# A decoder layer whose x and first weights arrive interleaved, and whose small loads leave POOL's queue

## The chip, the cores and the metric

The kernel runs on one core of a Trainium2 chip. The core's engines have instruction queues of their own: PE (TensorE, matrix multiply, with its weight loads shown as PEld), DVE (VectorE), ACT (ScalarE), POOL (GpSimd) and SP (SyncE, which here only issues transfers). All transfers run on the core's 16 DMA engines. The metric is the device time of one execution in microseconds; lower is better.

## The reference

One layer over 256 positions of width 1024, in float32. The input is normed and multiplied with one wide matrix; its columns are the queries, keys and values of three kinds of attention and three gates. The attention outputs are projected, gated, summed, projected again and added to x; then come a second norm and an MLP with a short convolution.

```
h = rmsnorm(x, ln1);  z = h @ w_in
qa, ka, va, qb, kb, vb, fb, qc, kc, vc, ga, gb, gc = split(z)
o_a = block-sparse attention(qa, ka, va) with a position bias
o_b = forgetting attention(qb, kb, vb, fb + b_f)
o_c = sliding-window attention(qc, kc, vc, sinks) with a position bias
x = x + (sigmoid(ga)*(o_a @ w_pa) + sigmoid(gb)*(o_b @ w_pb) + sigmoid(gc)*(o_c @ w_pc)) @ w_o
u = causal_conv3(rmsnorm(x, ln2) @ w_up);  a, b = split(u)
out = rmsnorm(x + (silu(a) * b) @ w_down, ln_f)
```

## The kernel before

Each float32 product is made of three fast products: an operand is split into a high part, which ACT writes in the fast type, and a low part, the rest, which DVE subtracts; PE adds high times high, low times high and high times low. Weights come as pieces of up to 128 rows by 1024 columns (512 KB). The class `Weights` takes each piece through three steps, in the order of use: "load" (SP issues the transfer into one of five `raw` buffers), "hi" (ACT, L109) and "lo" (DVE, L116). A piece holds for 512 output columns two blocks of 128 of the contraction index. The first four pieces are cut finer.

The row norm is not applied to h before the first products. Their left operand is x, transposed and times the gain ln1, in eight blocks of 128 by 256 (`hThi` and `hTlo`, L308 to L314); the scale of the norm, computed from the untransposed x (`xt`) by four ACT squares (L276), a short chain on DVE and ACT and a product with a diagonal matrix (`diag`, L282, and PE's L289), is multiplied in as the results leave PSUM. The products follow each other as groups: first qB and kB (four pieces, L394), then v1 (values and forget logits of the B heads, three pieces, L243 to L245), then qA and kA (four pieces; the first is called m0 below), v2, qC and so on.

The order of the work around PE's products is written by a planner (`filler`, `step`): each product adds its cost to a running clock, and other tasks are put between the products when the clock reaches their time in the table `AT` (norm, positions, mm, gates and others). An engine runs its instructions in the order in which they are written. ACT and DVE splits stand some pieces ahead of the product that uses them.

At the start SP issues transposed x (`in_xT`) and the first four pieces by turns: the gain with block 0 of x, two quarters of the first piece, block 1 of x, the rest of the piece, then x by two blocks and weights by half pieces (L167 to L193). Transposed x lies in `G`, which later serves other purposes. POOL, having made three constant masks, issues five small loads (L218 to L222): the position bias table (`relx`, two parts, and `oneh`), the forget bias (`bfb`) and the sinks (`skb`). PE runs seven products of zeros until its first operands are there. At most eight of SP's transfers are under way at once, since each waits for the one eight before it.

Of the kernel before, what the change touches and what calls it, by code (L numbers as in the profile page):

```python
# [7 lines left out]
F32 = mybir.dt.float32  # L8
F32R = mybir.dt.float32r
# [46 lines left out]
class Weights:  # L56

    def __init__(self, nc, pool, pieces):  # L60
        self.nc, self.pool, self.pieces = nc, pool, pieces
        self.raw, self.parts = {}, {}
# [74 lines left out]


@with_exitstack
def hybrid_kernel(ctx: ExitStack, tc: tile.TileContext, x, xT, ln_f, w_main, w_v1, w_v2, b_f, sinks,  # L140
                  rel_bias, onehot, cols, out):
# [38 lines left out]
    load_x(2, 4)  # L180
    W.load_to(2)
    load_x(4, 6)
    W.load_to(3)
    load_x(6, 8)
    W.load_to(4)
    cv = const.tile([P, 192], F32, name="cv")[:, :4 * 2 * NF + KD]
# [60 lines left out]
    def small(shape, name, bufs=2):  # L247
        return act.tile([P] + shape, F32, name=name, tag=name, bufs=bufs)
# [73 lines left out]
    for _ in range(2):  # L322
        W.step("lo")
    W.step("hi")
    low()
    W.step("lo")
    for k in range(2, 8, 2):
        lows = [x_hi(k), x_hi(k + 1)]
        W.hi_to(k // 2 + 1)
        for low in lows:  # L330
            low()
        W.prep_to(k // 2 + 1)
# [6 lines left out]
    def spawn(task, when=0.0):  # L339
        tasks.append((when, task))  # L340
# [111 lines left out]
    def group_v1():  # L452
# [429 lines left out]
    for j in range(NF):  # L882
# [12 lines left out]
        hi = ml.tile([P, S], F32R, name="ah", tag="ah", bufs=TAIL + 2)  # L895
        lo = ml.tile([P, S], F32R, name="al", tag="al", bufs=TAIL + 2)
# [149 lines left out]
```

## Time and profile before

| | us |
|---|---|
| median of 3 runs (range) | 388.01 (387.05 to 389.1) |
| the profiled execution | 388.68 |
| its span, first to last instruction | 387.0 |
| PE busy | 377.2 (97%) |
| DVE, ACT, POOL busy | 287.7, 230.7, 8.0 |

The share of busy time is a mean over stages with different limits. In the chain each piece of time belongs to what the last instruction in the end waited for; where the chain is all PE, only fewer or faster matmuls shorten the program, and where it names a transfer or another engine, PE stood still. The granted clock is 1.00 at TensorE's higher level, 2.4 GHz, and 0.50 at its lower, 1.2 GHz. A row's duration of a matmul overlaps the next one's; the step from one to the next is what counts.

### The profile page before, as it was taken

How to read it: one execution, taken by the hardware profiler on the slowest of the kernel's cores; microseconds unless marked ns; L12 is line 12 of the kernel's file. 1: busy time of each engine (PE TensorE's matmuls, PEld its weight loads, DVE VectorE, ACT ScalarE, POOL GpSimd, SP SyncE). 2: the span in 40 equal slices, each digit the busy share in tenths (PEclk: the TensorE clock that was granted, in tenths of full speed). 3: DMA queues.
4: the chain of work that ended last, by engine and by line, in shares of the span. 5: the costliest groups of instructions: out<-in, count | busy, mean ns of one | idle time of the engine just before them, and what ended most of it. 6: DMA issues, size and time to landing. Idle time of an engine off the chain costs nothing.

```text
span 387.0 us, 6530 instructions
## 1 busy us (share of the span) xinstructions
PE 377.2 (97%) x2464; PEld 340.1 (88%) x2464; DVE 287.7 (74%) x540; ACT 230.7 (60%) x399; POOL 8.0 (2%) x20
## 2 busy tenths in 40 slices
PE   6999999999999999999999999999999999999993
PEld 6999999787887888888899999999999999999983
DVE  3785967574856717967778999878887878888745
ACT  4883464665757685336587767556655656656433
POOL 4010000000000000000000000000000000000000
PEclk9899999999999999999999999999999999999998
DMA  7999765344552637444736567655565556463002
GB/s 197 402 331 334 279 181 181 130 130 149 170 172 90 218 108 233 151 160 119 262 108 222 204 224 223 216 196 186 170 213 180 201 171 205 171 218 109 2 0 108
DMA packets 21374, 70.86 MB, mean 183 GB/s; under 512 B 2504, under 2 KB 3413, under 8 KB 21344
## 3 DMA queue, kind: packets, MB, share of 16 engines
q1 hardware_dynamic: 20448, 68.05, 52.1%
q0 software_dynamic: 752, 2.18, 1.7%
q8 instruction: 19, 0.31, 0.4%
q10 hardware_dynamic: 144, 0.23, 0.2%
q14 instruction: 11, 0.09, 0.1%
HBM read 69.38 MB, written 1.07 MB: 182 GB/s over the span
## 4 chain that ended last, share of the span: by engine, by line
PE 96%; DMA 1%; DVE 1%; SPq 0%; ACT 0%; issue 0%; DVEq 0%
PE s L834 16%; PE acc L243 16%; PE acc L244 15%; PE acc L245 15%; PE pt L834 8%; PE o L834 8%; PE acc L394 7%; PE pt L394 2%; PE s L619 2%; PE o L394 1%; DMA raw<-in_w_main 1%; PE s L566 1%; PE s L608 1%; PE s L301 0%; PE pt L566 0%; PE pt L773 0%
## 5 line engine op out<-in xcount | busy, mean ns | idle before, releaser
L116 DVE TENSOR_TENSOR wlo<-raw,whi 128x1024 fp32r<-128x1024 f32 (+4 forms) x131 | 150.3, 1161 | 17.4 <-ACT whi L109 17.4
L109 ACT ACTIVATE whi<-raw 128x1024 fp32r<-128x1024 f32 (+4 forms) x131 | 129.1, 1005 | 49.2 <-PE acc L244 24.6
L243 PE MATMUL acc<-whi,hThi 128*128 128x512 f32 (+2 forms) x160 | 61.3, 383 | 0.0
L244 PE MATMUL acc<-whi,hTlo 128*128 128x512 f32 (+2 forms) x160 | 59.8, 374 | 0.0
L245 PE MATMUL acc<-wlo,hThi 128*128 128x512 f32 (+2 forms) x160 | 59.8, 374 | 0.0
L834 PE MATMUL s<-oThi,whi 128*128 128x256 f32 x176 | 49.3, 281 | 0.0
L834 PE MATMUL s<-oThi,wlo 128*128 128x256 f32 x176 | 49.2, 280 | 0.0
L834 PE MATMUL s<-oTlo,whi 128*128 128x256 f32 x176 | 48.9, 280 | 0.0
L842 ACT ACTIVATE ya<-v,cv 128x256 f32<-128x256 f32 x22 | 13.3, 603 | 42.7 <-DVE v L839 42.7
L243 PEld LDWEIGHTS acc<-whi,hThi 128*128 128x128 f32 x160 | 30.1, 188 | 6.0 <-issue 1.3
L245 PEld LDWEIGHTS acc<-wlo,hThi 128*128 128x128 f32 x160 | 30.0, 188 | 5.1
L244 PEld LDWEIGHTS acc<-whi,hTlo 128*128 128x128 f32 x160 | 30.1, 188 | 4.7 <-DVE hTlo L295 0.2
L244 PE MATMUL acc<-whi,al 128*128 128x512 f32 (+1 forms) x88 | 33.8, 384 | 0.0
L245 PE MATMUL acc<-wlo,ah 128*128 128x512 f32 (+1 forms) x88 | 33.8, 384 | 0.0
L243 PE MATMUL acc<-whi,ah 128*128 128x512 f32 (+1 forms) x88 | 33.8, 384 | 0.0
L834 PEld LDWEIGHTS s<-oTlo,whi 128*128 128x128 f32 x176 | 33.5, 191 | 0.0
L834 PEld LDWEIGHTS s<-oThi,wlo 128*128 128x128 f32 x176 | 33.0, 188 | 0.4
L834 PEld LDWEIGHTS s<-oThi,whi 128*128 128x128 f32 x176 | 33.0, 188 | 0.4
L834 PE MATMUL pt<-oThi,whi 128*128 128x256 f32 x88 | 24.8, 282 | 0.0
L834 PE MATMUL pt<-oThi,wlo 128*128 128x256 f32 x88 | 24.7, 281 | 0.0
L834 PE MATMUL pt<-oTlo,whi 128*128 128x256 f32 x88 | 24.7, 281 | 0.0
L834 PE MATMUL o<-oThi,whi 128*128 128x256 f32 x88 | 24.7, 281 | 0.0
(243 smaller groups left out, 749.0 us busy)
## 6 DMA issues: line engine op xcount, KB each, us to landing
raw<-in_w_main SPq DMA_DIRECT2D x115, 512.0 KB, 3.8
raw<-in_w_main SPq DMA_DIRECT2D x7, 256.0 KB, 5.6
raw<-in_w_v SPq DMA_DIRECT2D x4, 384.0 KB, 3.9
xt<-in_x SPq DMA_DIRECT2D x2, 512.0 KB, 6.9
G<-rowsd POOLq DMA_DIRECT2D x1, 1024.0 KB, 12.6
raw<-in_w_v SPq DMA_DIRECT2D x2, 390.0 KB, 6.2
G<-in_xT SPq DMA_DIRECT2D x3, 256.0 KB, 6.1
out_y<-xt SPq DMA_DIRECT2D x2, 288.0 KB, 2.2
```

The source lines that it names most:

```text
L109: self.nc.scalar.activation(self.parts[i][0][:, cs], self.raw[i][:, cs], AF.Copy)
L116: self.nc.vector.tensor_sub(lo[:, cs], self.raw[i][:, cs], hi[:, cs].bitcast(F32))
L243: nc.tensor.matmul(o, lh, rh, start=start, stop=False, **kw)
L244: nc.tensor.matmul(o, ll, rh, start=False, stop=False, **kw)
L245: nc.tensor.matmul(o, lh, rl, start=False, stop=stop, **kw)
L394: nc.tensor.matmul(o, w[:, kk, cs], hT[h][:, k, :], start=first, stop=last, skip_group_check=True)
L566: nc.tensor.matmul(sc[2 * i + e][:, lo:lo + m], q[h, qi, qs], k[h, ki, 0:m], start=True, stop=True)
L608: nc.tensor.transpose(pts[h][:, i * P:(i + 1) * P], L[:, h, i * P:(i + 1) * P], ident)
L619: nc.tensor.matmul(os[i][e * HD:(e + 1) * HD, cs], v[t][:, vi, e, :], p[:, S:ROWS] if t else p[:, 0:S], start=t == 0, stop=t == 1, **kw)
L834: nc.tensor.matmul(u, w, h2T[h][:, k, :], start=k == 0 and i == 0, stop=k == KD - 1 and i == 2)
L842: nc.scalar.activation(y, v, AF.Identity, scale=w[2], bias=w[3])
```

## The change

The host packs gain, transposed x and the first four pieces into one array `head`: 8 columns of gain, then four blocks of 1536 columns, each x block 2i, piece i, x block 2i+1. SP loads it in nine transfers into a buffer `begin` of its own, cut at columns 512, 1024, 1536 and then every 768. The pieces count as loaded, so the five `raw` buffers are free for what follows. The bias table becomes one array `table` of 34 rows, and bias and sinks are further columns of `cols`; SP loads both, and POOL none at the start. ACT and DVE take x and weights block by block. The norm's start in the table `AT` is 5.5 instead of 1.59, its product's 18.0 instead of 14.0, the gates' 20.0 instead of 18.2. oThi and oTlo become one tile; h2T takes the same tile 48 columns further on; some paddings change. The rest of the order stays.

```diff
-AT = dict(norm=1.59, positions=9.23, out0=26.0, out1=20.0, gates=18.2, sums=23.0,
-          fours=(37.46, 53.0, 68.5, 83.5), mm=14.0)
+AT = dict(norm=5.5, positions=9.23, out0=26.0, out1=20.0, gates=20.0, sums=23.0,
+          fours=(37.46, 53.0, 68.5, 83.5), mm=18.0)
...
+        self.raw, self.parts = dict(enumerate(pieces[:loaded])), {}
+        self.done["load"] = sum(i < loaded for i, _ in self.steps)
...
+    at.tile([P, 56], F32, name="pad3")
+    begin = at.tile([P, 8 + 4 * 1536], F32, name="begin")
+    W = Weights(nc, wpool, [begin[:, i, S:S + 1024] for i in range(4)] + v1 + main[0:4] + v2
+                + main[4:], 4)
...
-    nc.sync.dma_start(first, xT[:, 0:KD + S])
-    for _ in range(2):
-        W.step("load")
...
-    load_x(1, 2)
-    W.load_to(1)
-    load_x(2, 4)
-    W.load_to(2)
...
+    cuts = [0, 512, 1024, 1536] + [768 * i for i in range(3, 9)]
+    nc.sync.dma_start(at_start, head[:, 0:KD + cuts[1]])
+    for a, b in zip(cuts[1:], cuts[2:]):
+        nc.sync.dma_start(begin_flat[:, a:b], head[:, KD + a:KD + b])
...
+    W.load_to(5)
+    nc.sync.dma_start(tab, table)
+    W.load_to(7)
     for t in range(2):
         nc.sync.dma_start(xt[:, t, :], x[t * P:(t + 1) * P, :])
-    W.load_to(7)
     nc.sync.dma_start(cv, cols)
...
-    nc.gpsimd.dma_start(relx[0:NBUCKET, :], rel_bias)
-    nc.gpsimd.dma_start(oneh, onehot[:, 0:ROWS])
-    nc.gpsimd.dma_start(relx[32:34, :], onehot[32:34, ROWS:ROWS + 12])
-    nc.gpsimd.dma_start(bfb, b_f.to_broadcast([P, 4]))
-    nc.gpsimd.dma_start(skb, sinks.to_broadcast([P, 8]))
...
     W.step("hi")
     low()
+    W.step("lo")
     W.step("hi")
-    low = x_hi(1)
-    for _ in range(2):
+    W.step("lo")
+    for k in range(1, 8):
+        low = x_hi(k)
+        W.step("hi")
+        low()
         W.step("lo")
...
-    oT = [act.tile([P, 8, S], F32R, name=n, tag=n, bufs=1) for n in ("oThi", "oTlo")]
+    oT = parts_T(0)
...
-    h2T = [act.tile([P, KD, S], F32R, name=n, tag=n, bufs=1) for n in ("oThi", "oTlo")]
+    h2T = parts_T(48)
```

On SP, the transfers issued from the program's start to m0, before; `in_w_main` 128x256 and 128x512 are parts of the first four pieces, `in_w_v` is v1, 128x1024 of `in_w_main` is m0 and its followers:

```order
L170 DMA G<-in_xT 128x264
L104 DMA raw<-in_w_main 128x256 x2
L175 DMA G<-in_xT 128x256
L104 DMA raw<-in_w_main 128x512
L175 DMA G<-in_xT 128x512
L104 DMA raw<-in_w_main 128x512 x2
L175 DMA G<-in_xT 128x512
L104 DMA raw<-in_w_main 128x512 x2
L175 DMA G<-in_xT 128x512
L104 DMA raw<-in_w_main 128x512 x2
L104 DMA raw<-in_w_v 128x780 x2
L191 DMA xt<-in_x 128x1024 x2
L104 DMA raw<-in_w_v 128x520
```

And now:

```order
L187 DMA begin<-in_head 128x520
L189 DMA begin<-in_head 128x512 x2
L189 DMA begin<-in_head 128x768 x6
L105 DMA raw<-in_w_v 128x780
L198 DMA tab<-in_table 34x396
L105 DMA raw<-in_w_v 128x780
L105 DMA raw<-in_w_v 128x520
L201 DMA xt<-in_x 128x1024 x2
L202 DMA cv<-in_cols 128x196
L105 DMA raw<-in_w_main 128x1024 x4
```

x and the first pieces are nine transfers instead of fifteen, all of v1 is issued ahead of `xt`, and the table stands between its first two parts; ahead of m0 stands otherwise what stood there before.

On ACT, from the last split of the first four pieces to m0's, before; `whi<-raw` is a split (780 and 520 columns: v1, 1024: m0 and the next), `G,ss<-xt` are the squares, `nr` is the norm's scale:

```order
L109 ACTIVATE whi<-raw 128x512 x2
L109 ACTIVATE whi<-raw 128x780 x2
L276 ACTIVATE G,ss<-xt 128x512 x4
L109 ACTIVATE whi<-raw 128x520
L255 ACTIVATE nr<-nv 128x2
L256 ACTIVATE nr<-nr 128x2
L109 ACTIVATE whi<-raw 128x1024 x2
```

And now:

```order
L310 ACTIVATE hThi<-begin 128x256
L110 ACTIVATE whi<-begin 128x512
L110 ACTIVATE whi<-raw 128x780 x2
L110 ACTIVATE whi<-raw 128x520
L110 ACTIVATE whi<-raw 128x1024
L273 ACTIVATE G,ss<-xt 128x512 x4
L252 ACTIVATE nr<-nv 128x2
L253 ACTIVATE nr<-nr 128x2
L110 ACTIVATE whi<-raw 128x1024
```

m0's split stands ahead of the four squares now, where it stood behind the norm's scale.

On DVE, the subtractions around the norm, before; `nv` to `diag` are the norm's chain, 128x1024 is m0 and the next:

```order
L116 TENSOR_TENSOR wlo<-raw,whi 128x512 x2
L116 TENSOR_TENSOR wlo<-raw,whi 128x780 x2
L253 SCALAR_TENSOR_TENSOR nv<-ss 128x2
L265 TENSOR_TENSOR nt<-nr 128x2
L266 TENSOR_TENSOR nt<-nt,nv 128x2
L267 TENSOR_SCALAR nt<-nt 128x2
L269 TENSOR_TENSOR nq<-nr,nt 128x2
L282 TENSOR_SCALAR diag<-ident,nq 128x128 x2
L116 TENSOR_TENSOR wlo<-raw,whi 128x520
L116 TENSOR_TENSOR wlo<-raw,whi 128x1024 x4
```

And now:

```order
L117 TENSOR_TENSOR wlo<-begin,whi 128x512
L117 TENSOR_TENSOR wlo<-raw,whi 128x780 x2
L117 TENSOR_TENSOR wlo<-raw,whi 128x520
L250 SCALAR_TENSOR_TENSOR nv<-ss 128x2
L262 TENSOR_TENSOR nt<-nr 128x2
L263 TENSOR_TENSOR nt<-nt,nv 128x2
L264 TENSOR_SCALAR nt<-nt 128x2
L266 TENSOR_TENSOR nq<-nr,nt 128x2
L279 TENSOR_SCALAR diag<-ident,nq 128x128 x2
L117 TENSOR_TENSOR wlo<-raw,whi 128x1024 x4
```

The last part of v1 moves ahead of the norm's chain; m0's subtraction stays right behind it.

## Rows read from the trace of the kernel before

**Rows 1.** The page's part 4: the chain by engine, shares of the span.

```profile
PE 96%; DMA 1%; DVE 1%; SPq 0%; ACT 0%; issue 0%; DVEq 0%
```

**Rows 2.** Busy us by stretch (PE, PEld, DVE, ACT, POOL), PEclk, DMA share, GB/s.

```profile
6.82:8.57 1.75, 0.00 (x1) 0.01 (x1) 0.32 (x2) 0.69 (x2) 0.00 (x0) 1.00 0.89 286
9.50:12.91 3.41, 3.41 (x17) 3.41 (x17) 3.18 (x7) 2.87 (x7) 0.58 (x1) 0.50 1.00 378
53.00:380.50 327.50, 327.27 (x2116) 292.07 (x2114) 249.44 (x463) 197.13 (x340) 0.56 (x1) 1.00 0.49 164
```

**Rows 3.** Timeline of PE, 0 to 9 us: start, us, operation, [idle before].

```profile
4.38 0.80 PE L394 MATMUL pt<-hThi,whi 128*128 128x256 f32 x2
...
8.57 0.39 PE L394 MATMUL pt<-hThi,whi 128*128 128x256 f32 x1 [1.75 <-ACT whi L109]
```

**Rows 4.** The chain in order of time: start us, us, what.

```profile
2.63 5.24 DMA raw<-in_w_main
...
9.29 1.07 PE pt L394 x4
10.36 1.28 PE o L394 x6
...
13.68 0.72 PE pt L394 x6
...
21.81 0.12 PE acc L243
...
25.74 0.45 PE s L289 x4
...
27.98 7.90 PE acc L394 x66
...
202.16 2.73 PE pt L834 x24
...
224.16 5.65 PE s L834 x48
```

**Rows 5.** DMA issues: engine, count, KB each, us from issue to landing.

```profile
G<-in_xT SPq DMA_DIRECT2D x1, 132.0 KB, 2.6
...
raw<-in_w_main SPq DMA_DIRECT2D x1, 256.0 KB, 5.2
...
raw<-in_w_main SPq DMA_DIRECT2D x1, 512.0 KB, 7.2
```

**Rows 6.** Stretches by their transfers; the last two columns are DMA share and GB/s.

```profile
1.50:3.50 2.00, 2.00 (x11) 2.00 (x11) 0.04 (x1) 0.57 (x1) 1.86 (x6) 1.00 0.85 182
3.50:4.50 1.00, 1.00 (x6) 0.79 (x5) 0.96 (x3) 0.59 (x2) 1.00 (x3) 1.00 0.69 133
4.50:9.75 5.25, 3.28 (x17) 2.87 (x18) 2.34 (x6) 2.56 (x7) 0.87 (x2) 0.98 0.95 272
9.75:20.00 10.25, 10.25 (x71) 9.59 (x70) 7.60 (x13) 8.77 (x21) 0.58 (x1) 0.85 1.04 401
```

**Rows 7.** Timeline of POOL.

```profile
10.75 0.58 POOL L224 TENSOR_SCALAR skn<-skb 128x8 f32<-128x8 f32 x1 [5.38 <-DMA skb<-in_sinks]
```

**Rows 8.** Timeline of DVE: a block's subtractions, and the one behind the norm.

```profile
13.56 0.87 DVE L314 SCALAR_TENSOR_TENSOR hTlo<-G,hThi 128x256 fp32r<-128x256 f32 x2
14.35 1.28 DVE L116 TENSOR_TENSOR wlo<-raw,whi 128x512 fp32r<-128x512 f32 x2
...
22.20 2.96 DVE L116 TENSOR_TENSOR wlo<-raw,whi 128x520 fp32r<-128x520 f32 x3
```

**Rows 9.** Timeline of ACT: a block's splits, the first square, m0's split.

```profile
12.83 0.91 ACT L313 ACTIVATE hThi<-G 128x256 fp32r<-128x256 f32 x2
13.65 1.16 ACT L109 ACTIVATE whi<-raw 128x512 fp32r<-128x512 f32 x2
...
17.48 0.63 ACT L276 ACTIVATE G<-xt 128x512 f32<-128x512 f32 x1 [0.48 <-DMA xt<-in_x]
...
21.00 1.06 ACT L109 ACTIVATE whi<-raw 128x1024 fp32r<-128x1024 f32 x1
```

More of the change, by code (lines that the diff above doesn't have):

```diff
@@ L56, with __init__ @@
 class Weights:
-    def __init__(self, nc, pool, pieces):
+    def __init__(self, nc, pool, pieces, loaded):
         self.nc, self.pool, self.pieces = nc, pool, pieces
-        self.raw, self.parts = {}, {}
+        self.raw, self.parts = dict(enumerate(pieces[:loaded])), {}
         self.steps = [(i, cs) for i, p in enumerate(pieces) for cs in self.spans(i, p.shape[1])]
         self.done = dict.fromkeys(("load", "hi", "lo"), 0)
+        self.done["load"] = sum(i < loaded for i, _ in self.steps)
         self.more = None
@@ L139, in hybrid_kernel @@
 @with_exitstack
-def hybrid_kernel(ctx: ExitStack, tc: tile.TileContext, x, xT, ln_f, w_main, w_v1, w_v2, b_f, sinks,
-                  rel_bias, onehot, cols, out):
+def hybrid_kernel(ctx: ExitStack, tc: tile.TileContext, x, head, ln_f, w_main, w_v1, w_v2, table,
+                  cols, out):
     nc = tc.nc
@@ L155, in hybrid_kernel, with parts_T @@
     G = act.tile([P, 3, 2, D], F32, name="G")
+    def parts_T(offset):
+        t = act.tile([P, 2 * KD * S + 48], F32R, name="oT", tag="oT", bufs=1)
+        t = t[:, offset:offset + 2 * KD * S].rearrange("p (h k s) -> p h k s", h=2, s=S)
+        return [t[:, 0], t[:, 1]]
+    attn_ctx = ExitStack()
+    at = attn_ctx.enter_context(tc.tile_pool(name="attn", bufs=1))
     main = [w_main[i] for i in range(w_main.shape[0])]
@@ L159, in hybrid_kernel @@
     v2 = [w_v2[i] for i in range(w_v2.shape[0])]
-    W = Weights(nc, wpool, main[0:4] + v1 + main[4:8] + v2 + main[8:])
+    at.tile([P, 56], F32, name="pad3")
+    begin = at.tile([P, 8 + 4 * 1536], F32, name="begin")
+    at_start = begin[:, 0:KD + 512]
+    gain1, begin = begin[:, 0:KD], begin[:, KD:].rearrange("p (i c) -> p i c", i=4)
+    W = Weights(nc, wpool, [begin[:, i, S:S + 1024] for i in range(4)] + v1 + main[0:4] + v2
+                + main[4:], 4)
     nxt = [0]
@@ L167, in hybrid_kernel @@
     nc.scalar.preload_act_table_set("natural_log_exp_and_others")
-    xTr = G[:, 0].rearrange("p t (k s) -> p (t k) s", s=S)
-    first = G[:, 1, 0, 0:KD + S]
-    nc.sync.dma_start(first, xT[:, 0:KD + S])
-    for _ in range(2):
-        W.step("load")
-    def load_x(k0, k1):
-        nc.sync.dma_start(xTr[:, k0:k1, :].rearrange("p k s -> p (k s)"),
-                          xT[:, KD + k0 * S:KD + k1 * S])
-    load_x(1, 2)
-    W.load_to(1)
-    load_x(2, 4)
-    W.load_to(2)
[L182 to L186, printed above, removed]
+    begin_flat = begin.rearrange("p i c -> p (i c)")
+    x_at = [begin[:, k // 2, (k % 2) * 1280:(k % 2) * 1280 + S] for k in range(KD)]
+    cuts = [0, 512, 1024, 1536] + [768 * i for i in range(3, 9)]
+    nc.sync.dma_start(at_start, head[:, 0:KD + cuts[1]])
+    for a, b in zip(cuts[1:], cuts[2:]):
+        nc.sync.dma_start(begin_flat[:, a:b], head[:, KD + a:KD + b])
+    cv = const.tile([P, 208], F32, name="cv")[:, :4 * 2 * NF + KD + 12]
+    tab = const.tile([34, 12 + ROWS], F32, name="tab")
     const.tile([P, 48], F32, name="pad0")
     ln2 = cv[:, 8 * NF:8 * NF + KD]
-    W.load_to(6)
+    bfb, skb = (cv[:, a:b] for a, b in ((4 * 2 * NF + KD, 4 * 2 * NF + KD + 4),
+                                        (4 * 2 * NF + KD + 4, 4 * 2 * NF + KD + 12)))
+    relx, oneh = tab[:, 0:12], tab[:, 12:]
+    W.load_to(5)
+    nc.sync.dma_start(tab, table)
+    W.load_to(7)
     for t in range(2):
         nc.sync.dma_start(xt[:, t, :], x[t * P:(t + 1) * P, :])
-    W.load_to(7)
     nc.sync.dma_start(cv, cols)
@@ L308, in x_hi @@
     def x_hi(k, on_vector=False):
-        src, sc = (xTr[:, k] if k else first[:, KD:]), first[:, k:k + 1]
+        src, sc = x_at[k], gain1[:, k:k + 1]
         if on_vector:
@@ L319, in hybrid_kernel @@
     low()
+    W.step("lo")
     W.step("hi")
-    low = x_hi(1)
-    for _ in range(2):
-        W.step("lo")
[L324 to L332, printed above, removed]
+    W.step("lo")
[3 more added lines that the diff above has]
+        low()
+        W.step("lo")
     rs = {}
@@ L485, in hybrid_kernel @@
     lf, cum = small([8], "lf", 1), small([16], "cum", 1)[:, :8]
-    act.tile([P, 16], F32, name="pad1")
+    act.tile([P, 32], F32, name="pad1")
     def fox(logits):
@@ L990 @@
     perm_c = np.concatenate([np.arange(h * HD, (h + 1) * HD) for h in heads_c])
+    xT, w0 = tiles(a["x"][0].T, 1), tiles(w_in[:, 768:1280], 2)
+    head = [a["ln1"][0].reshape(KD, P).T]
+    for i in range(4):
+        head += [xT[2 * i], w0[i], xT[2 * i + 1]]
     main = [
-        tiles(w_in[:, 768:1280], 2),
         tiles(w_in[:, 0:512], 2),
@@ L1012 @@
     dist = np.arange(ROWS) - (P - 1)
-    onehot = np.zeros((34, ROWS + 12), np.float32)
+    table = np.zeros((34, 12 + ROWS), np.float32)
+    table[0:NBUCKET, 0:12] = a["rel_bias"]
     b = _buckets(ROWS)[np.maximum(dist, 0)]
-    onehot[b, np.arange(ROWS)] = 1.0
-    onehot[32, :ROWS] = dist < 0
-    onehot[33, :ROWS] = dist >= 128
-    onehot[32, ROWS:] = NEG
-    onehot[33, ROWS + 4:] = NEG
+    table[b, 12 + np.arange(ROWS)] = 1.0
+    table[32, 12:] = dist < 0
+    table[33, 12:] = dist >= 128
+    table[32, 0:12] = NEG
+    table[33, 4:12] = NEG
     cw = a["conv_w"][0].reshape(3, 2 * NF, P)
@@ L1023 @@
                            a["ln2"][0].reshape(KD, P)], 0).T
+    cols = np.concatenate([cols, np.broadcast_to(a["b_f"], (P, 4)),
+                           np.broadcast_to(a["sinks"], (P, 8))], 1)
     arrays = {
         "x": a["x"][0],
-        "xT": np.concatenate([a["ln1"][0].reshape(KD, P).T, tiles(a["x"][0].T, KD)[0]], 1),
+        "head": np.concatenate(head, 1),
         "ln_f": a["ln_f"][None],
@@ L1030 @@
         "w_v2": tiles(np.concatenate([w_in[:, 512:768], w_in[:, 2180:2308]], 1), 2),
-        "b_f": a["b_f"],
-        "sinks": a["sinks"],
-        "rel_bias": a["rel_bias"],
-        "onehot": onehot,
+        "table": table,
         "cols": cols,
```

8 lines of the change are left out of this document (1 added, 7 removed).

## The prediction

> **What bounds the kernel now.** I read the chain of waits on the page first, then the busy times by stage, then the chain over the first 30 us, then the transfers. The chain is 96% PE [rows 1], and between 53 and 380.5 us PE is busy 327.27 of 327.50 us [rows 2]. Nothing that the other engines do there is worth time. What can be won lies before 53 us and in the last 6 us, which the change does not touch. At the start the reader is to see three things. PE begins real work at 4.38 us and then sits idle for 1.75 us until a split weight block comes [rows 3]. That block's transfer is the piece of the chain that lasts 5.24 us [rows 4], and it landed 5.2 us after its issue, where a transfer of half the size landed in 2.6 [rows 5]. And after the pause the granted clock is 0.50, the lower of the two levels, from 9.50 to 12.91 us [rows 2]: the six matmuls of a block take 1.28 us instead of 0.72 [rows 4].
>
> **The reason for the late block.** From 4.50 to 9.75 us the transfers moved 272 GB/s at a DMA busy share of 0.95; from 9.75 to 20 us 401 GB/s at 1.04 [rows 6]. The five small POOL transfers are in flight in the first of these stretches: POOL's first use of the last of them, 4 KB, starts at 10.75 us after 5.38 us of waiting [rows 7]. Between 3.50 and 4.50 us the rate is only 133 GB/s. I take this as contention with POOL's transfers, though the trace does not prove it.
>
> **The change part by part.**
>
> Start. The first transfer is 260 KB instead of 132 KB, and it holds x's block 0 and the first 256 weight columns. The old one landed 2.6 us after 0.79, at 3.4; the additional 128 KB at 182 to 401 GB/s [rows 6] are 0.3 to 0.7 us, so about 3.8. DVE's first split and ACT's run side by side as before, and PE starts at about 4.3: nothing won or lost against 4.38 [rows 3]. Block 0 has the same 12 matmuls; their last ends at 6.82 [rows 2], is issued some 0.3 us earlier, since a matmul's row overlaps the next, and so near 6.5 in both kernels.
>
> Block 1. It needs the third transfer, 0.79 MB in all. From 3.4 us (135,000 bytes landed) the other 0.66 MB take 1.6 us at 401 GB/s, 2.4 at 272, 3.6 at 182: landed at 5.0, 5.8 or 7.0. I take 5.3, near the fast end, since POOL is gone from the queues and the rows are 2 KB. Then ACT splits x (0.91 us for two) and the weights (1.16 for two) [rows 9], and DVE subtracts (1.28 for two, [rows 8]): the high half is ready 1.0 us after landing, the low half 1.7 us, at 7.0. PE comes to that third matmul at about 6.8, so it runs at about 7.05; before it ran at 9.29 [rows 4]. Saved: 2.2 us (0.5 to 2.5 by the three rates).
>
> Blocks 2 to 7. PE takes two times 0.72 us per block [rows 4]. ACT takes (0.91 + 1.16)/2 = 1.04 us, DVE (0.87 + 1.28)/2 = 1.08 us, and a block of 384 KB takes 0.98 us at 401 GB/s, 1.45 at 272. All keep pace, so the finer order of the splits costs nothing; its cover is gone if the rate stays at 272.
>
> Clock. Without the 1.75 us pause I expect no fall at 9.50. 3.41 us at half speed are 1.7 us of work: saved 1.7. Together 3.9 us: the v1 group, which starts at 21.81 us [rows 4], starts at 17.9. It lasts until 27.98 less the 0.45 us of L289, which the change moves behind it: PE reaches the next group's first piece (m0, the first 512 KB piece of w_main) at 23.6 instead of 27.5, and its third matmul, the first to need m0's low half, at about 23.85.
>
> The new wait. m0 is issued behind everything else of the start: 5.94 MB (head 3.15, v1 1.07, table 0.05, x 1.05, columns 0.10, m0 0.52). The first transfer's 2.6 us less 0.3 for its bytes leave 2.3 us that are fixed, so m0 lands at 0.79 + 2.3 + 5.94/0.401 = 17.9 us; before it was issued at 13.68 and landed 7.2 later, at 20.9 [rows 5]. PE moves up by 3.9 us, the transfer by 3.0. Worse, ACT now splits m0 ahead of the four squares of the norm, and DVE's subtraction for m0 stands behind the norm's last step (diag). So 1.06 us for the split, then, as before from the first square (17.48, [rows 9]) to DVE's next subtraction (22.20, [rows 8]), 4.7 us, then 1.1 us of subtraction (three take 2.96, the first of them a short one): ready at 17.9 + 6.9 = 24.8. PE waits 24.8 - 23.85 = 0.95 us, where before it had 4 us to spare. Behind that wait stand all of PE's later matmuls. Bounds: the wait is gone if m0 lands by 16.9, for which the bytes would have to move at 430 GB/s; if m0 lands as late as before, at 20.9, it is 3.95. I take 0.95, near the rate of the 10 us after 9.75.
>
> In the table's transfer I count 0.13 us, its 54 KB at 401 GB/s. The Trainium skill (DMA: Bandwidth & Descriptors, section on why a DMA increments its semaphore by 16) says that the number of DMA engines used is the largest up to 16 that divides the outer count. For the table's 34 rows that is 2, and no run here shows it. By it two engines carry 17 rows of 1,584 bytes each, an estimate of 1.07 us at a sixteenth of 401 GB/s, and m0 would land at 18.9.
>
> POOL. Its five issues go; what needs the data comes late: the table at L360's matmul at about 16.5 us against a landing near 12.5, the gate bias at the end of v1, the sinks after 68 us. Nothing on the path, and if the table came late PE would wait for it directly.
>
> Addresses. oT, h2T and the tiles of the last pool move by some hundred bytes. The trace has 528 matmuls of L834 at two speeds, 2.73 us for 24 and 5.65 for 48 [rows 4], 0.114 and 0.118 us each. If the move sets the faster one for all, 2 us are won; if it sets the 0.120 of L394, 1 us is lost. I take 0, since most stand at 0.118 now and the buffers keep their distance from the weights.
>
> Sum: 2.2 + 1.7 - 0.95 = 2.95 us off 388.68 us, the profiled execution's own time (span 387.0): 385.7. That execution is 0.67 us above the median of the three runs, 388.01; against the median it would be 385.1. The new wait is paced by transfers and not by when PE began, so the times should lie together; I take 385.5. The Trainium skill (TensorE: Matmul & The Clock Gate, Part 1) says that the moment at which the clock is released is not tied to the kernel's start and varies from run to run. The runs' range, 387.05 to 389.1, agrees with it; by it a run of before without the fall would gain only 1.25 us, which also ends near 385.7.
>
> **The rivals.**
>
> No new wait. If the chain of m0 is shorter than I add up, or PE arrives later by itself, all of the 3.9 us stays: 388.68 - 3.9 = 384.8, or 384.1 from the median; about 384.3. For it: the diag's wait and the squares could overlap where I add them. Against: on ACT m0's split stands ahead of the squares, in a fixed order.
>
> The pause comes back elsewhere. PE idle for one or two us at 24 us is much like the pause of 1.75 us that was followed by the lower clock. If it falls again, 1.7 us is lost once more: 387.2.
>
> The change doesn't quicken the start. The rate is low already from 1.50 to 3.50 us, at 182 GB/s [rows 6], when no small transfer was yet moving; if that is the state of the memory at the start and not POOL's doing, block 1 comes at 8 us again, the pause and the low clock stay, and the time is about 388.0.
>
> Slower. The mechanism is the line on ACT and DVE in front of m0: m0 lands where it did, at 20.9, its low half is ready at 27.8, PE idles 3.95 us and eats the whole gain of 3.9, and the clock falls behind so long a pause: 388.68 + 1.8 = 390.4. With the fall it decides from m0 landing at 19.2 on. For it: the same 5.4 MB still go ahead of m0, so only a faster start can bring it forward. Against: the slow stretch of before cost some 1.7 us alone (5.25 us at 272 instead of 401 GB/s).
>
> **How the numbers follow.** The main case has 0.42, no new wait 0.20, the pause come back 0.13, no quicker start 0.13, slower 0.12. The measurement can tell 0.5%, or 1.94 us, from no change: faster means under 386.07, slower over 389.95. Of the main case (384.5 to 386.5) some 0.32 lies under 386.07, of no new wait all, of the third 0.02: faster 0.54. Slower: most of the last case and little else, 0.11. The rest, 0.35, is the same. The range runs from 383.7 (no new wait, and some gain from the addresses) to 388.6.
>
> **What would show it.** Right: one PE stream from about 4.3 us with no pause over 0.5 us before 17 us, no stretch at 0.50 in the granted clock, near 400 GB/s from 4 us on, v1 starting near 18 us, and a PE wait of about 1 us for DVE's subtraction near 24 us. Wrong: a pause before block 1, a rate under 300 GB/s with POOL's loads gone, m0 landing after 19 us, a wait of over 2 us at m0, or other steps of L834's matmuls.

## Result and the profile after

The changed kernel takes 390.66 us (median of seven runs, 389.98 to 391.78) against 388.41 us for the kernel before on the same chips; the ratio is 1.0082, 95% interval 1.0064 to 1.0100. I had forecast 385.5 us, faster, in a range of 383.7 to 388.6. The direction was wrong and the time lies outside the range. The profiled execution took 390.34 us, with a span of 388.6.

**The start.** Stretches of the changed kernel, columns as in [rows 6]; the first four answer to those rows, the last two are new.

```profile
1.50:3.50 2.00, 2.00 (x11) 2.00 (x11) 0.00 (x0) 0.57 (x1) 0.95 (x4) 1.00 0.81 213
3.50:4.50 1.00, 1.00 (x7) 1.00 (x6) 0.86 (x3) 0.42 (x1) 0.00 (x0) 1.00 0.79 257
4.50:9.75 5.25, 3.53 (x18) 2.83 (x18) 2.94 (x7) 3.19 (x7) 0.00 (x0) 0.85 1.00 359
9.75:20.00 10.25, 10.25 (x75) 9.48 (x74) 7.56 (x13) 6.31 (x12) 0.23 (x1) 0.91 1.04 395
8.00:11.60 3.60, 3.53 (x15) 3.24 (x16) 3.57 (x8) 3.60 (x9) 0.00 (x0) 0.53 1.03 405
24.50:27.50 3.00, 3.00 (x25) 2.82 (x25) 2.79 (x8) 3.00 (x4) 0.73 (x1) 1.00 0.02 6
```

From 4.50 to 9.75 us the transfers now move 359 GB/s, not 272, so that part came as forecast. But between 8.0 and 11.6 us the granted clock is low as it was before between 9.50 and 12.91 [rows 2], and between 24.5 and 27.5 us next to nothing is transferred, at 6 GB/s. The kernel before moved 302 GB/s between 22 and 28 us.

PE's timeline of the changed kernel, with the idle time before a row in brackets, answers to [rows 3]:

```profile
4.12 0.77 PE L386 MATMUL pt<-hThi,whi 128*128 128x256 f32 x2
...
8.06 0.50 PE L386 MATMUL pt<-hThi,whi 128*128 128x256 f32 x1 [1.54 <-ACT whi L110]
...
8.79 0.58 PE L386 MATMUL pt<-hThi,wlo 128*128 128x256 f32 x1
...
36.01 0.36 PE L500 MATMUL s<-lf,tri 128*128 128x4 f32 x2 [0.66 <-DVE lf L497]
...
43.34 0.72 PE L520 MATMUL s<-cumrows,pick 8*128 8x256 f32 x4 [0.51 <-DVE cumrows L516]
```

The pause before block 1 is 1.54 us instead of 1.75. Block 1's third matmul runs at 8.79 us (9.29 before [rows 4]), the v1 group starts at 20.88 (21.65 in the timeline of before). So PE is 0.77 us ahead there, not 3.9. Then come two waits that the kernel before does not have: 0.66 us before the running sums of `lf`, the logarithms of the B heads' forget gates (L500), and 0.51 before L520, which copies these sums to all partitions. At L558, the first scores, PE is 0.96 us behind (54.08 against 53.12).

The chain in order of time (start us, us, what) shows what stands behind these waits:

```profile
12.99 7.12 DMA raw<-in_w_main
20.22 1.06 ACT whi L110
21.28 2.46 ACT G L273 x8
...
25.69 1.07 DVE wlo L117
...
28.07 4.06 DMA raw<-in_w_v
32.23 0.85 ACT whi L110
...
35.69 0.18 DVE lf L497
36.01 0.36 PE s L500 x2
...
42.88 0.41 DVE cumrows L516
43.34 0.72 PE s L520 x4
```

The chain no longer runs along PE there. It goes from m0's landing at 20.11 us (7.12 after its issue, 7.2 before [rows 5]) through ACT's split, the squares (L273), DVE's norm and subtraction of m0 (to 26.91) and of the next piece (to 28.05), a transfer of w_v2 that could only be issued at 28.07, and that piece's split to lf at 35.69, and so to PE's L500.

ACT's timeline of the changed kernel, 15 to 34 us, answers to [rows 9]:

```profile
20.22 1.06 ACT L110 ACTIVATE whi<-raw 128x1024 fp32r<-128x1024 f32 x1 [3.50 <-DMA raw<-in_w_main]
21.18 0.61 ACT L273 ACTIVATE G<-xt 128x512 f32<-128x512 f32 x1
...
23.54 0.19 ACT L273 ACTIVATION_READ_ACCUMULATOR G<-xt 128x1 f32 x1
...
32.23 0.85 ACT L110 ACTIVATE whi<-raw 128x768 fp32r<-128x768 f32 x1 [1.23 <-DMA raw<-in_w_v]
```

DVE's, to the last of [rows 8]:

```profile
23.76 0.16 DVE L250 SCALAR_TENSOR_TENSOR nv<-ss 128x2 f32<-128x2 f32 x1 [5.96 <-ACT G L273]
...
25.69 3.49 DVE L117 TENSOR_TENSOR wlo<-raw,whi 128x1024 fp32r<-128x1024 f32 x3
```

SP's, which issues the transfers; the last line is the kernel before's, for the same four pieces:

```profile
12.99 4.55 SPq L105 DMA_DIRECT2D raw<-in_w_main  x4
17.82 11.71 SPq L105 DMA_DIRECT2D raw<-in_w_v  x4
...
22.97 3.68 SPq L104 DMA_DIRECT2D raw<-in_w_v  x4
```

The reader is to see three things. ACT idles 3.50 us for m0, though x has landed at 17.26 and 18.57 us and its squares could run; in the order of the changed kernel they stand behind m0. DVE idles 5.96 us for those squares, with m0's subtraction queued behind the norm. And SP needs 11.71 us for the four issues of w_v2 (3.68 us in the kernel before, from 22.97 on), because all but the first take a raw buffer that one of DVE's subtractions of m0 to m2 must free. That is the transfer gap at 24.5.

**After 54 us** PE's lag stays at 0.9 to 1.1 us until 198 us, grows to 1.38 by 214 and stays there to PE's last matmul. Between 202 and 214 us the matmuls of L826 (L834 before) follow each other every 0.118 us, in the profiled execution of before every 0.114 [rows 4]. From the start of PE's last matmul to the end it is 7.05 us instead of 6.78; the ten traces of the changed loads have 6.99 to 7.06 there, the four of the old ones 6.70 to 6.78. No run shows where these 0.3 us come from, and I had taken it that the change doesn't touch the end.

### The profile page after: what moved, and what is told of

Its sections match the earlier page's. It is cut to its first block, busy times and chain, and to the rows that moved or that the text cites. A ratio compares the mean times of both kernels' runs of the same rounds, so it can differ in the third digit from the quotient of the medians.

```text
span 388.6 us, 6509 instructions
## 1 busy us (share of the span) xinstructions
PE 377.7 (97%) x2464; PEld 340.1 (88%) x2464; DVE 287.2 (74%) x540; ACT 230.3 (59%) x399; POOL 5.0 (1%) x15
## 3 DMA queue, kind: packets, MB, share of 16 engines
HBM read 69.38 MB, written 1.07 MB: 181 GB/s over the span
## 4 chain that ended last, share of the span: by engine, by line
PE 88%; DMA 5%; DVE 2%; ACT 2%; SPq 1%; issue 1%; DVEq 0%; ACTq 0%
PE s L826 16%; PE acc L240 15%; PE acc L241 14%; PE acc L242 14%; PE pt L826 8%; PE o L826 8%; PE acc L386 5%; DMA begin<-in_head 2%; DMA raw<-in_w_main 2%; PE s L611 2%; DVE wlo L117 1%; DMA raw<-in_w_v 1%; PE s L558 1%; SPq L189 1%; ACT whi L110 1%; PE s L600 1%
## 5 line engine op out<-in xcount | busy, mean ns | idle before, releaser
L117 DVE TENSOR_TENSOR wlo<-raw,whi 128x1024 fp32r<-128x1024 f32 (+3 forms) x122 | 144.7, 1200 | 15.4 <-ACT whi L110 15.3
L110 ACT ACTIVATE whi<-raw 128x1024 fp32r<-128x1024 f32 (+3 forms) x122 | 123.9, 1037 | 48.0 <-PE acc L241 21.8
L826 PE MATMUL s<-oT,whi 128*128 128x256 f32 x352 | 64.2, 281 | 0.0
L826 PEld LDWEIGHTS s<-oT,whi 128*128 128x128 f32 x352 | 54.8, 190 | 0.3
L826 PE MATMUL s<-oT,wlo 128*128 128x256 f32 x176 | 49.3, 281 | 0.0
L834 ACT ACTIVATE ya<-v,cv 128x256 f32<-128x256 f32 x22 | 13.3, 603 | 42.9 <-DVE v L831 42.9
L826 PEld LDWEIGHTS s<-oT,wlo 128*128 128x128 f32 x176 | 33.1, 188 | 0.4
L826 PE MATMUL pt<-oT,whi 128*128 128x256 f32 x176 | 33.0, 281 | 0.0
L826 PE MATMUL o<-oT,whi 128*128 128x256 f32 x176 | 32.9, 281 | 0.0
L826 PEld LDWEIGHTS pt<-oT,whi 128*128 128x128 f32 x176 | 27.8, 190 | 0.3
L826 PEld LDWEIGHTS o<-oT,whi 128*128 128x128 f32 x176 | 27.8, 190 | 0.0
L826 PE MATMUL pt<-oT,wlo 128*128 128x256 f32 x88 | 24.7, 281 | 0.0
L826 PE MATMUL o<-oT,wlo 128*128 128x256 f32 x88 | 24.7, 281 | 0.0
```

Source lines behind the costliest of these rows:

```text
L110: self.nc.scalar.activation(self.parts[i][0][:, cs], self.raw[i][:, cs], AF.Copy)
L117: self.nc.vector.tensor_sub(lo[:, cs], self.raw[i][:, cs], hi[:, cs].bitcast(F32))
L826: nc.tensor.matmul(u, w, h2T[h][:, k, :], start=k == 0 and i == 0, stop=k == KD - 1 and i == 2)
L834: nc.scalar.activation(y, v, AF.Identity, scale=w[2], bias=w[3])
```

## Experiments

Ratios are to the kernel before, from runs on one chip. Where PE's lead or lag is given, it is a matmul's start in the profiled execution against the same matmul in that of before.

**e1_old_times.** The three due times back, nothing else:

```diff
-AT = dict(norm=5.5, ..., gates=20.0, ..., mm=18.0)
+AT = dict(norm=1.59, ..., gates=18.2, ..., mm=14.0)
```

> The changed kernel with the three due times norm, gates and mm put back to 1.59, 18.2 and 14.0; loads and splits stay as changed. Theory now (order): the changed kernel loses its time between 20 and 44 us because the squares of the norm stand behind m0's split on ACT, so the norm, DVE's subtractions behind it and the release of the raw buffers come late, the four pieces of w_v2 land at 30 to 36 us, and PE waits 0.66 us before the sums (L500) and 0.51 us before L520. Then with the old times both waits go: the four pieces land before 31 us, L520 starts near 41.7 us (43.34 changed, 42.38 before), and the time is some 1.7 us under the changed kernel's 390.66, near 389 or less, ratio to before 0.997 to 1.003. Rival (transfers): m0 lands at 20.1 us whatever the order, and the pieces behind it are late by that; then the waits stay and the ratio is 1.006 to 1.010.

Measured: 387.06 us, ratio 0.9984 (0.9970 to 0.9997). PE has no wait after 8.15 us; its lead is 2.63 us at L558. The times alone cost the changed kernel 0.0098 of 387.6, 3.8 us, more than its whole loss (the two ratios are from different chips). m0 landed at 20.26 us and no wait came of it, so the rival (transfers) is out. ACT in this run:

```profile
17.45 0.63 ACT L273 ACTIVATE G<-xt 128x512 f32<-128x512 f32 x1 [1.09 <-DMA xt<-in_x]
...
19.36 0.61 ACT L273 ACTIVATE G<-xt 128x512 f32<-128x512 f32 x1
...
20.83 1.99 ACT L110 ACTIVATE whi<-raw 128x1024 fp32r<-128x1024 f32 x2
```

The squares fill the time in which ACT waited for m0.

**e6_before_new_times.** The reverse, on the kernel before:

```diff
-AT = dict(norm=1.59, ..., gates=18.2, ..., mm=14.0)
+AT = dict(norm=5.5, ..., gates=20.0, ..., mm=18.0)
```

> The kernel before with nothing but the three new due times (norm 5.5, gates 20.0, mm 18.0). Theory (order): squares behind m0's split put the norm, the release of the raw buffers and the pieces of w_v2 late here too; m0 lands near 20.9 us and its low half is ready near 27.8, where PE comes at about 27.4, then waits of 0.5 to 1.2 us before the sums and L520: 1.0 to 2.5 us slower, ratio 1.003 to 1.007. Rival (the times fit only the new loads or do no harm without them): ratio 0.999 to 1.001.

Measured: 392.62 us, ratio 1.0122 (1.0099 to 1.0145), twice what I expected of it. PE's waits after 9 us (total us, times, longest):

```profile
PE acc L394 <- DVE wlo L116: 2.3, 1, 2.3
PE s L508 <- DVE lf L505: 1.9, 1, 1.9
```

The order does its harm with the old loads too.

**e8_norm_only.** One of the three:

```diff
-AT = dict(norm=5.5,
+AT = dict(norm=1.59,
```

> The changed kernel with one due time put back, norm to 1.59; gates and mm stay at 20.0 and 18.0. Theory (the squares' place is what holds everything): all of the gain of the old times comes with it, ratio 0.997 to 1.001; the row copy and the gates, which stand behind the third piece of w_v2 on ACT, cost at most 0.3 us more at the sums. Rival (gates and mm matter as much): ratio 1.002 to 1.006, with a wait before L500 left.

Measured: 387.07 us, ratio 0.9980 (0.9965 to 0.9995); no wait before L500. gates and mm cost nothing.

**e12_one_place.** m0's split goes behind the four squares and the two short steps of the norm's scale; on DVE the norm's first step goes ahead of v1's last piece. Nothing else changes its place on any engine:

```diff
-AT = dict(norm=5.5,
+AT = dict(norm=4.0,
```

> The changed kernel with norm at 4.0 in place of 5.5; gates and mm stay at 20.0 and 18.0. On ACT this exchanges one pair: the four squares come right ahead of m0's split in place of right behind it (with 1.59 they stood further forward, ahead of the last piece of w_v1); the splits of m1 to m3 and all behind it stay. Theory (the squares wait in line for m0's landing at 20.1 us, though x is there by 18.6): the squares run near 17.3 to 19.9 us, DVE's m0 subtraction ends near 23.5 instead of 26.9, the four pieces of w_v2 land before 31 us, and the whole loss goes: ratio 0.997 to 1.000. Rival (the norm as a whole must come earlier, or the gates' place matters): only part goes, ratio 1.002 to 1.006.

Measured: 386.43 us, ratio 0.9974 (0.9958 to 0.9990). ACT's timeline, 15 to 34 us:

```profile
17.62 0.63 ACT L273 ACTIVATE G<-xt 128x512 f32<-128x512 f32 x1 [0.56 <-DMA xt<-in_x]
...
20.05 0.18 ACT L273 ACTIVATION_READ_ACCUMULATOR G<-xt 128x1 f32 x1
...
20.81 2.06 ACT L110 ACTIVATE whi<-raw 128x1024 fp32r<-128x1024 f32 x2
```

DVE's:

```profile
21.85 0.48 DVE L279 TENSOR_SCALAR diag<-ident,nq 128x128 f32<-128x128 f32 x2
22.25 6.36 DVE L117 TENSOR_TENSOR wlo<-raw,whi 128x1024 fp32r<-128x1024 f32 x6
```

SP's:

```profile
12.38 5.50 SPq L105 DMA_DIRECT2D raw<-in_w_main  x4
21.14 4.95 SPq L105 DMA_DIRECT2D raw<-in_w_v  x4
```

The squares end by 20.23 us instead of 23.73, the norm's diag by 22.3, and w_v2 is issued from 21.14 us on. PE waits for nothing after 9 us, although m0 landed at 20.45 us, later than in the changed kernel. This one exchange is worth the whole loss; with the squares ahead, m0's landing at 20.45 us costs nothing.

**e3_filler.** Three matmuls on zeros between block 0 and block 1:

```diff
         for kk in range(nk):
+            if nxt[0] == 1 and kk == 1:
+                for _ in range(3):
+                    nc.tensor.matmul(wps, warm, warm, start=True, stop=True)
```

> The changed kernel with three more matmuls on zeros (128x128, as the seven at the start) between block 0 and block 1, some 1.4 us of work in the pause of 1.54 us. Theory (the pause lets the clock fall): the granted clock stays at 1.00, block 1 to 3 run at 0.12 instead of 0.21 us a step, the v1 group starts at 19.3 instead of 20.88 us. Nothing is gained at the end, since the chain through m0 sets L500: PE waits longer there, and the ratio stays at 1.005 to 1.009. Rival (PE's own time decides): the 1.6 us stay, ratio 1.004. Rival (the clock falls by itself at that time): clock 0.50 between 8 and 12 us as before, ratio 1.008.

Measured: 390.48 us, ratio 1.0071 (1.0055 to 1.0087). The clock does not fall, v1 starts at 18.74 us, 2.1 us earlier than in the changed kernel, and PE's waits after 9 us are:

```profile
PE acc L389 <- DVE wlo L117: 2.1, 1, 2.1
PE s L503 <- DVE lf L500: 0.8, 1, 0.8
PE s L523 <- DVE cumrows L519: 0.3, 1, 0.3
```

PE gains 2.1 us and pays them back at m0; the span, 388.4 us, is that of the changed kernel. So there the transfer and split chain sets the time, not PE's start, as the first theory had it; the fall of the clock has no part in the changed kernel's loss that these runs can tell (390.48 without it, 390.66 with it in the trace).

**e5_filler_old_times.** The edits of e1 and e3 together.

> The changed kernel with the old due times (norm 1.59, gates 18.2, mm 14.0) and the three filler matmuls in the pause between block 0 and block 1. Theory (the fall of the clock and the order are the two losses): the clock stays at 1.00, the v1 group starts at 18.7 us, m0's low half is ready near 23.7 us, before PE comes to it, and nothing waits before 54 us; PE is 2.9 us ahead of before there, and every run has this, not only those whose pause happened to be short. Time 385.2 to 386.2, ratio 0.992 to 0.996 (old times alone: 0.9984). Rival (transfers set the end): PE waits at m0 and at the pieces of w_v2 as much as it gained, ratio 0.998.

Measured: 386.81 us, ratio 0.9968 (0.9954 to 0.9982). The mechanism is as expected (v1 at 18.86 us, no wait over 0.16 us behind block 1), the gain about half of it. Against e3 it differs in the three times alone: v1 starts within 0.12 us, neither trace has a low clock in the start, and 0.0103 of 387.6, 4.0 us, lies between them (ratios from two chips). It is the version that beats both kernels most clearly; e12 stands within its interval.

**e4_hold_back.** The fourth transfer waits until the second has landed:

```diff
     for a, b in zip(cuts[1:], cuts[2:]):
+        if a == 1536:
+            nc.gpsimd.tensor_copy(begin_flat[:, 1536:1537], begin_flat[:, 1023:1024])
         nc.sync.dma_start(begin_flat[:, a:b], head[:, KD + a:KD + b])
```

> The changed kernel, but the fourth transfer of the start and all behind it are issued only when the second has landed (a copy of one column by GpSimd into the fourth's space makes them wait). Theory (transfers in flight share the engines): the third transfer, for block 1, now lands near 6.9 us because the fourth, fifth and sixth move 0.6 MB beside it; alone with the second it lands at 5.5 to 6.0 us, and block 1 begins at 7.0 instead of 8.06. The fourth then lands near 8.0 us and later ones some 0.5 us later than now. Rival (the engines are slow for the first microseconds whatever is in flight): the third lands at 6.7 to 7.0 us still, block 1 begins at 8 us, and later transfers are 1 us or more late. The time says little: ratio 1.005 to 1.012.

Measured: 392.63 us, ratio 1.0138 (1.0113 to 1.0162). ACT's first splits of blocks 1 and 2 in the changed kernel:

```profile
6.98 0.51 ACT L310 ACTIVATE hThi<-begin 128x256 fp32r<-128x256 f32 x1 [1.49 <-DMA begin<-in_head]
...
7.93 0.51 ACT L310 ACTIVATE hThi<-begin 128x256 fp32r<-128x256 f32 x1
```

and with the hold:

```profile
5.41 0.51 ACT L312 ACTIVATE hThi<-begin 128x256 fp32r<-128x256 f32 x1 [0.23 <-DMA begin<-in_head]
...
8.74 0.51 ACT L312 ACTIVATE hThi<-begin 128x256 fp32r<-128x256 f32 x1 [2.30 <-DMA begin<-in_head]
```

The third transfer is there for ACT at 5.41 us instead of 6.98, and PE goes from block 0 to block 1 with no pause over 0.32 us. The fourth comes at 8.74 (7.93 changed), PE waits 1.05 us for it, and m0 lands at 22.05 and makes PE wait 2.82 us, so the time was worse than I expected.

**e11_hold_one.** Old times, one filler matmul, and the hold only until the first has landed; shown against e4:

```diff
-            nc.gpsimd.tensor_copy(begin_flat[:, 1536:1537], begin_flat[:, 1023:1024])
+            nc.gpsimd.tensor_copy(begin_flat[:, 1536:1537], begin_flat[:, 511:512])
```

> The changed kernel with the old due times, the fourth transfer and those behind it issued only when the first has landed (3.5 us; in the run above it was the second), and one filler matmul between block 0 and block 1. Theory (transfers in flight share the engines): the third lands near 6.0 us, block 1 begins at 7.0 to 7.3, the fourth lands near 7.9 us, in time for block 2, and the v1 group starts at 18.2 to 18.6 us, 0.2 to 0.5 us before that of the kernel with filler alone (18.7 to 18.9); ratio 0.995 to 0.997. Rival (what is won at block 1 is lost at block 2 again, as with the longer hold): PE waits 0.5 us or more before block 2 or 3, ratio 0.997 to 0.999.

Measured: 387.10 us, ratio 0.9987 (0.9975 to 0.9999). The last of the 2 KB packets (second and third transfer) moves at 5.1 us; in the eight runs of these loads without a hold it is at 5.4 to 6.5. But PE waits 0.40 and 0.22 us before block 2 and v1 starts at 19.41: what is won at block 1 is lost at block 2, as the rival had it.

**e7_pool_loads_back.** Old times, and five loads of the old sizes on GpSimd's queue into a part of G that nobody reads:

```diff
+    D0 = G[:, 2, 0]
+    nc.gpsimd.dma_start(D0[0:32, 0:12], table[0:32, 0:12])
+    nc.gpsimd.dma_start(D0[0:34, 16:16 + ROWS], table[:, 12:])
+    nc.gpsimd.dma_start(D0[32:34, 0:12], table[32:34, 0:12])
+    nc.gpsimd.dma_start(D0[:, 512:516], table[0:1, 0:4].to_broadcast([P, 4]))
+    nc.gpsimd.dma_start(D0[:, 520:528], table[0:1, 4:12].to_broadcast([P, 8]))
```

> The changed kernel with the old due times, and five small loads on GpSimd's queue again (same rows and bytes as before, into a place that nobody reads). Theory of the prediction (contention): the rate between 4.5 and 9.75 us falls from some 360 GB/s towards 272, the third transfer lands 0.9 us or more later, near 7.5 us, and block 1 begins near 8.5 to 9.0. Rival (the slow start is not these loads' doing): the third transfer lands between 6.4 and 7.2 us as in the runs so far, blocks 2 to 7 at most 0.4 us later. Ratio 0.998 to 1.003 by the rival, 1.003 to 1.006 by the theory.

Measured: 389.56 us, ratio 1.0034 (1.0015 to 1.0054), ten runs from 387.79 to 391.46. Stretches (the last column is GB/s):

```profile
4.50:9.75 5.25, 4.51 (x26) 4.04 (x25) 3.10 (x7) 3.08 (x7) 0.87 (x2) 1.00 1.01 305
8.00:10.00 2.00, 1.78 (x14) 1.58 (x13) 1.51 (x4) 1.89 (x4) 0.00 (x0) 1.00 1.07 196
10.00:12.00 2.00, 2.00 (x17) 2.00 (x18) 0.90 (x2) 0.17 (x1) 0.00 (x0) 1.00 0.84 243
```

and in e1:

```profile
4.50:9.75 5.25, 3.96 (x27) 3.27 (x26) 3.47 (x8) 3.56 (x8) 0.00 (x0) 1.00 0.97 338
8.00:10.00 2.00, 1.85 (x15) 1.85 (x16) 1.88 (x5) 2.00 (x6) 0.00 (x0) 1.00 1.02 378
```

Neither side had it right. Block 1 is not touched: it begins at 7.50 us (7.42 in e1). But while the two broadcasts are moved, in packets of 128 and 256 bytes that take up to 2.08 us each, the rate falls to 196 GB/s where e1 moved 378, the sixth transfer lands at 13.94 instead of 9.52 us, and PE waits 2.25 us for it at 15.04, after which its clock falls once more. The profiled execution is the slowest of the ten, 1.9 us above their median, so a usual one must lose less.

**e9_before_pool_moved.** The kernel before with only GpSimd's loads moved into the table and the columns, as in the change:

```diff
+    W.load_to(5)
+    nc.sync.dma_start(tab, table)
     W.load_to(6)
...
-    nc.gpsimd.dma_start(relx[0:NBUCKET, :], rel_bias)
...
-    nc.gpsimd.dma_start(skb, sinks.to_broadcast([P, 8]))
```

> The kernel before with one part of the change: GpSimd's five small loads go into the table's transfer (behind the first piece of w_v1) and into the columns; x, weights, splits and due times stay as before. Theory (the broadcasts on GpSimd's queue hold single engines for 0.3 to 2 us, and this alone is what the start gains): blocks 2 to 7 come on time, rate between 4.5 and 9.75 us 340 GB/s or more instead of 272, while block 1 still begins near 8 us after a pause of 1.2 to 1.7 us; ratio 0.995 to 0.998, as good as the changed loads with the old times (0.9984). Rival (interleaved loads in 2 and 3 KB rows are the gain): the rate stays under 300 GB/s and the ratio at 0.999 to 1.001.

Measured: 387.92 us, ratio 1.0009 (0.9993 to 1.0025): nothing, against my theory. The rate stayed under 300 GB/s, as the rival had it:

```profile
4.50:9.75 5.25, 4.27 (x25) 3.72 (x25) 3.04 (x7) 3.37 (x7) 0.00 (x0) 1.00 0.93 291
```

The 12 runs fall in two groups, six from 386.88 to 387.34 us with a mean clock of 0.995 to 0.998 and six from 388.49 to 389.26 with 0.991 to 0.994; the profiled one is of the first and shows no fall.

**e10_before_pool_moved_filler.** The same with the three filler matmuls of e3.

> As the run before, with three filler matmuls on zeros between block 0 and block 1 to keep the clock. Theory: no stretch at 0.50 in the granted clock, 1.0 to 1.7 us under the kernel with the loads moved alone in those runs in which the clock would fall; ratio 0.993 to 0.996, equal to or better than the changed kernel with old times and filler (0.9968). Rival (interleaving matters): 0.997 to 1.000.

Measured: 387.44 us, ratio 0.9995 (0.9984 to 1.0005), the rival's figure. The upper group is gone: 11 runs from 387.07 to 388.00. A pause of 1.50 us behind the filler stayed, and no fall followed.

**e2_table_48_rows.** The table padded to 48 rows:

```diff
-    tab = const.tile([34, 12 + ROWS], F32, name="tab")
+    tab = const.tile([48, 12 + ROWS], F32, name="tab")
-    relx, oneh = tab[:, 0:12], tab[:, 12:]
+    relx, oneh = tab[0:34, 0:12], tab[0:34, 12:]
...
-    table = np.zeros((34, 12 + ROWS), np.float32)
+    table = np.zeros((48, 12 + ROWS), np.float32)
```

> The changed kernel with the table's transfer of 48 rows (14 of zeros) in place of 34; nothing else differs. The 34 packets of 1,584 bytes pass between 12.25 and 13.75 us, 67 ns each and never more than 8 in 0.25 us, which is what two engines can do. Theory (two engines): those two stay some 1.1 us behind for every transfer that follows, so with 48 rows over more engines m0 lands near 19.0 instead of 20.11 us, and as the chain through m0 sets the waits before L500 and L520, the time falls by 0.5 to 1.1 us, ratio 1.004 to 1.007. Rival (bytes only): 22 KB more at 400 GB/s, m0 lands at 20.1 to 20.2 us and the ratio stays at 1.008.

Measured: 391.12 us, ratio 1.0083 (1.0060 to 1.0106), no gain. In the profiled execution, the slowest of the four, at most 6 of the table's packets are in flight at once, 3 with 34 rows; m0 lands at 21.27 us, not sooner: the last four of the columns' packets move at 18.9 to 19.2 us, right behind a 16 KB packet of instructions that takes 1.10 us. So it does not show what the row count is worth.

## Why the prediction was wrong

**The step that failed is the new wait, and the gain that I set against it failed by as much.** The mechanism of the wait was right: m0's split ahead of the squares, DVE's subtraction behind the norm, low half ready 6.8 us after landing (26.91 - 20.11) where I had 6.9. Its price was not. I gave it 0.95 us; the same order costs 3.8 us by e1, 4.2 by e12 (0.0108 of 387.3), 4.0 between e3 and e5, and 4.7 in the kernel before (e6, 0.0122). In e3, where PE comes early as I had it, PE waits 2.07 us at m0 and 1.07 at two places behind it, so two parts were missing from my sum.

First, m0 lands at 20.1 us (20.1 to 21.3 in the runs with these loads and neither hold nor GpSimd's loads), not at 17.9. With 20.1 my own sum gives 2.2 us for e3's PE, which comes to m0's third matmul at 24.84 us. The lower rate, 359 and not 401 GB/s between 4.50 and 9.75 us, is the smaller reason: the 5.94 MB that I counted had been moved by 18.5 us. But by m0's landing 6.6 MB had, since packets of later transfers move beside m0's.

Second, I stopped at PE's first wait. I did not ask who waits for DVE besides PE: SP does, for the raw buffers, and behind SP three of the four pieces of w_v2, and behind their splits on ACT the row copy and the gates. In the changed kernel PE comes to m0 so late (26.59 us) that the first wait is a mere 0.14 us, and it still loses 1.17 us to the second half of the line. That the buffers carry the delay on is read from the chain and SP's issues; no run changed their number. My slower rival had the time almost exactly, 390.4, but by luck and at the wrong place: it wanted 3.95 us of idle PE at m0 and a fall of the clock behind them.

**Block 1 and the clock, 3.9 us, were sized on one execution.** In the profiled execution of the changed kernel block 1 gained 0.5 us, the lower end of my bounds, and the clock fell again. In others it did not: e1, e8 and e12, the same loads, had pauses of 0.77, 0.72 and 0.31 us and no fall, and led by 2.6 to 2.9 us at L558. Yet by the medians of e1 and e12 the loads are worth only 0.6 to 1.0 us. Of the lead at L558, 0.4 us goes between 202 and 214 us, where the profiled execution of before has its quicker steps, and 0.3 behind PE's last matmul. Most of the rest lies in that execution: 388.68 us with a clock of 0.993 is not typical; of the 92 runs of the kernel before beside the experiments 33 take 388.1 to 389.1 us with a mean clock of 0.992 to 0.994, the others, but for one, 386.8 to 387.8 with 0.994 to 0.998. So I subtracted 1.7 us for a fall that nearly two runs in three do not seem to have. That the slower group is the one with the fall is taken from its clock and from e10, where filler removes it; only one execution of before was traced. The Trainium skill (TensorE: Matmul & The Clock Gate, Part 1) says that the moment at which the clock is released varies from run to run; I had quoted it and then reckoned from the single execution all the same. The traces agree, and by more than I thought: PE's first matmul is at 1.1 us in all of them, and half-speed steps (0.213 us) turn to full ones between 4.6 us (e10) and 10.4 us (e2).

**Contention.** I took the slow stretch of before for the doing of GpSimd's loads, and block 1's delay for its result. The runs bear out neither. The rate from 4.50 to 9.75 us rose with the new layout and not with these loads gone: 272 GB/s before, 291 and 280 with them moved in the old layout (e9, e10), 338 to 361 with the changed loads and old or new times (e1, e12, changed), 305 with GpSimd's loads put back beside those (e7). And with them back block 1 stayed. Its transfer is late because later ones are in flight beside it: the last 2 KB packet moves at 5.0 and 5.1 us with these held back (e4, e11) and at 5.4 to 6.5 in the eight runs without. The Trainium skill (DMA: Bandwidth & Descriptors, Queues, rings and completion order) says that completion is not first in, first out for the engine that issues. No trace here shows that on SP's queue, where every transfer with a recorded landing landed in the order of issue; what the traces show is that transfers overlap. In the changed kernel the last 2 KB packet of the third transfer moves at 6.5 us, when 3 KB packets of the fourth and later ones have moved for 2.2 us. Counting bytes in order, as I did for the third transfer and for m0, came out too early by 1.6 and 2.2 us.

**What held.** PE starts at 4.12 us (4.3 forecast), GpSimd's issues are on no path, the finer order of the splits costs nothing (PE waits nowhere in blocks 2 to 7 of e1, e8 and e12 by more than 0.15 us), the pause at m0, of 0.14 us, brought no second fall in the changed kernel. Addresses don't set L834's steps: e6 has those of before and steps of 0.118 us where before has 0.114.

Together: 387.5 us less 0.6 for the loads plus 3.8 for the order (e1), or less 1.0 plus 4.2 (e12), is 390.7; 390.66 were measured. That is no check, since the order's price is the measured time less that of e1 or e12. With the order's price from e6, 4.7, the sum is 391.2 to 391.6, so the two effects add up to within 0.9 us.

Open: why moving GpSimd's loads gains nothing in the old layout (e9) while putting them back costs 0.5% in the new one (e7), why the steps were 0.114 us for a stretch of one execution, and the 0.3 us at the end.

## What to carry to other kernels

When a step is moved on an engine that works in order, follow the line behind it to its end, through the buffers it frees and the transfers that these let start, and price every waiter, not the first alone. A step whose input comes late belongs behind those whose input is there: one exchange on ACT was worth 1.1% here. When a transfer's landing decides a wait, add to its bytes those of the transfers behind it that are in flight: here 0.66 MB and 1.6 us in the profiled execution. And before a profiled execution's pause or slow clock is subtracted, look whether the other runs have it.

## Not expected of the hardware

- A broadcast of 16 or 32 bytes a row to 128 rows on GpSimd's queue is moved in packets of which one took up to 2.08 us (e7), and a 384 KB transfer beside it came 4.4 us late, in the slowest of ten executions; in the profiled execution of before the longest took 1.30 us.
- A pause of PE is not always followed by the lower clock: 1.54 us (changed), 1.75 (before), 1.94 (e6), 2.25 (e7) and 2.82 us (e4) were; 1.50 (e10, behind the filler), 1.88 (e2), 2.07 (e3) and a second one of 2.30 in e6 were not.
- The granted clock reads 1.00 before the first release, though the steps are those of half speed (e2, 4.3 to 10.4 us).
